# Expert v stage and FFN down projections with tokens stationary and 512 weight columns moving

## The chip, the cores and the metric

One core of one Trainium2 chip. The metric is the device time of one execution in microseconds (us), the median of several runs. A profile was taken of one further execution; in it all matrix work runs on PE (TensorE), elementwise work on DVE (VectorE), ACT (ScalarE) and POOL (GpSimd), and most transfers are issued by SP.

## What is computed

Two transformer blocks on 256 tokens of width 1024. The first has attention and then a PEER layer: for each token, 8 heads choose 16 of 16384 experts. The kernel computes it densely, as 128 groups of 128 experts:

```python
q = xc @ w_query; s = einsum(q, sub_keys); top-16 of each half, then top-16 of the sums
act = gelu(xc @ u_sel.T);   h = h + sum over chosen k of (g * act)[k] * v_sel[k]
```

The second block has a mixer (convolution, block attention, gated linear attention), a cross attention over 256 memory rows, and a gated FFN of width 2752 with a short convolution:

```python
x = x + hybrid_mixer(rmsnorm(x, norm_mix_g)); x = x + memory_cross_attention(rmsnorm(x), rmsnorm(mem))
x = x + conv_ffn(rmsnorm(x, norm_ffn_g))      # up, conv, silu(gate) * up, then @ w_down (2752 x 1024)
return rmsnorm(x, final_norm_g)               # x * rsqrt(mean(x * x) + eps) * gain
```

## The kernel before

**Units.** All weights come as units of 128 x 1024 fp32 numbers (512 KB). `unit()` loads one (`raw`), makes `wh`, its value rounded to fp32r (mostly on ACT), and `wl`, the rest (mostly on DVE; POOL in part of the u stage). Moving data is split in the same way (`ch`, `cl` or `ah`, `al`), and each product is three matmuls: high x high, high x low, low x high. There are 4 `raw` buffers and 3 each of `wh` and `wl`.

**Layout.** The residual `h1` lies by feature: 128 features on partitions, 8 feature blocks, 256 tokens along the free dimension. In most projections (`stat8`) a 128 x 128 weight block is stationary and 256 tokens move. A few (`by_token`: `mv`, `gv`, `go`) hold 128 tokens stationary and move the weight columns; for `mv` these are 512.

**Expert stages.** `u_unit(j)` computes one group's activations (24 matmuls). `v_unit(j)` multiplies them by the gates and adds their product with `v` to four PSUM banks, `acc`. A bank holds two feature blocks of 256 tokens; a v unit is 8 feature blocks of three matmuls, 24 in all. First 90 u units run, then pairs of v and u units for the other 38, then the last 90 v units. The gates of 8 groups are loaded at a time (`gate_load`, 1 MB).

**The joint.** After the last v unit four DVE instructions add `acc`, scaled by 1/2048, to `h1`; `gained` then makes `ah` and `al` from it (ACT and DVE, 8 each). In program order the memory's key and value projections (`xk`, `xv`) follow, then the norm's factor and the mixer's first projection, `glr`. `xk` and `xv` do not need `h1`.

**FFN.** 21 full steps `f` of two up units (`ua`, `ug`, 24 matmuls each) and, two steps later, the down unit `dn`, plus one half-filled step (`um`). `down_part` adds to four PSUM banks `facc` with the same form as `v_unit`. The last two down units run in parts, so that banks finish one after another.

**Tail.** Before: by feature, `facc` is added to `h1`, squared, summed over partitions by matmuls with a column of ones, turned into the root's inverse, spread over partitions by two transposes, multiplied with gain and factor, and stored in five pieces.

**Order.** Operations are recorded with priorities in program order (`fl.bias` shifts some), and `schedule()` places them by a greedy simulation with costs written in `_cost`; each engine then runs its own list in that order. All instructions are issued from one line (L681), so the profile is read by the names of tiles: `s` stands for every region of the areas s1, s2 and s3, `d`, `g`, `s`, `p` are also the names of the PSUM pairs, and `h` is `h1`.

Of the kernel before, what the change touches and what calls it, by code (L numbers as in the profile page):

```python
# [9 lines left out]
F32 = mybir.dt.float32  # L10
# [3 lines left out]
AF = mybir.ActivationFunctionType  # L14
OP = mybir.AluOpType
# [4 lines left out]
P = 128  # L20
NM = 16
T = 256
S = NM + T
D = 1024
KD = D // P
NEG = -1e30
FF = 2752
NF = 22
# [229 lines left out]
CST, EAR = {}, {}  # L258
# [4 lines left out]
        _o += _a.shape[1]  # L263


def _feat(x):

    return np.ascontiguousarray(x.T.reshape(KD, P, -1).transpose(1, 0, 2))


def pack(i):
    u = _units(i)
    st = np.empty((len(PLAN), P, 8, P), np.float32)
    for j, (name, m) in enumerate(PLAN):
        st[j] = u[name][m].reshape(P, 8, P)
    ks = i["peer_sub_keys"][0].reshape(16, P, P).transpose(2, 0, 1)
    c, e = _consts()
    return {
        "st": st,
        "xt": _feat(np.concatenate([i["meta_tokens"], i["x"][0]], 0)),  # L280
        "mt": _feat(i["mem_2"][0]),
        "sk": np.ascontiguousarray(ks),
        "vec": np.concatenate([a for _, a in _vec_list(i)], 1),
        "cst": np.concatenate(list(c.values()), 1),
        "ear": np.concatenate(list(e.values()), 1),
    }


# [403 lines left out]
def _build(tc, nc, ctx, A, O):  # L692
    fl = Flow(tc, nc)
    PE, V, SC, G, Q = fl.pe, fl.v, fl.s, fl.g, fl.q
# [18 lines left out]
    cst = one([P, A["cst"].shape[1]], F32, "cst")  # L713
    eps = one([P, 2], F32, "eps")
    h1 = one([P, KD, T], F32, "h1")
# [42 lines left out]
    def v_(name, j=0, n=1, rows=slice(None)):  # L758
        o = VEC[name][0] + j
        return vec[rows, o:o + n]  # L760

    def c_(name, rows=slice(None)):
        o, n = CST[name]
        return cst[rows, o:o + n]

    ident = c_("ident")

    def sm(n=8):
        return fl.tile([P, 32], F32, "sm")[:, :n]

    def bank(tag, name=None):
        return fl.tile([P, 512], F32, tag, name)
# [115 lines left out]
    r1, r2, r3 = area("s1"), area("s2"), area("s3", F32R)  # L888
# [9 lines left out]
    tmp = r2(4416)  # L898
    mask = r2(S)
    ear = tmp[:, 0:EAR["mask"][0]]  # L900
# [14 lines left out]
    mq = r1(8, T, back=0)  # L915
    old = r1.at[0]
    mk = r1(8, S)
# [14 lines left out]
    Q.dma_start(cst[:, :nc_], A["cst"][:, :nc_])  # L932
    pre.append(unit("kr"))
    Q.dma_start(ear, A["ear"][:, 0:EAR["mask"][0]])
    Q.dma_start(mask, A["ear"][:, EAR["mask"][0]:])
    oc = [bank("d")[:, :S] for j in range(2)]
    for j in range(2):
        stat8(oc[j], pre[j], nh, nl, ALL, True)
# [1 line left out]
    o = bank("g")  # L940
    total(o, squares(x, S, KD, 2), VC)
    r = sm(12)
# [22 lines left out]
    for half in range(2):  # L965
        a, b = slice(64 * half, 64 * half + 64), slice(64 - 64 * half, 128 - 64 * half)
# [511 lines left out]
    def v_unit(j, lo="v"):  # L1478
        if j == 0:
            acc.extend(bank(tag, "acc") for tag in "sspp")  # L1480
        if j % 8 == 0 and j < P - 16:
            gate_load(j // 8 + 2)
        if j % 2 == 0:
            g, e = divmod(j, 8)
            for i in range(2):
                a = slots(j + i).rearrange("p (b t) -> p b t", (P, NB16, 16), b=NB16)
                V.tensor_tensor(a, a, loaded[g][:, e + i], op=OP.mult)
        a = slots(j)
        ch, cl = fl.tile([P, T], F32R, "ch"), fl.tile([P, T], F32R, "cl")
        split(a, ch, cl)  # L1490
        wh, wl = unit("v", lo=lo)
        for d in range(8):
            o = acc[d // 2][:, (d % 2) * T:(d % 2 + 1) * T]
            PE.matmul(o, wh[:, d], ch, start=j == 0 and d % 2 == 0, stop=False, skip_group_check=True)
            PE.matmul(o, wh[:, d], cl, start=False, stop=False, skip_group_check=True)
            PE.matmul(o, wl[:, d], ch, start=False, stop=j == P - 1 and d % 2 == 1, skip_group_check=True)

    class Side:

# [58 lines left out]
    qz, at_ = r1(1024), r1(1024)  # L1558
    FULL = slice(0, T)

    for i in range(4):
        a = h1[:, 2 * i:2 * i + 2]
        V.scalar_tensor_tensor(a, acc[i].rearrange("p (a b) -> p a b", (P, 2, T), a=2), 1.0 / 2048, a, op0=OP.mult, op1=OP.add)
        for k in (2 * i, 2 * i + 1):
            gained(h1[:, k], v_("mix", k), ah[:, k], al[:, k])
    for j in range(2):
# [236 lines left out]
    SC.activation(rsb, rep, AF.Copy)  # L1803
    fl.bias -= BIAS[2]
    facc = [bank(tag, "facc") for tag in "sspp"]

    def up(name, dst, j, tag):

# [10 lines left out]

    held, down = {}, {}  # L1820

    def down_part(f, ds):
        ch, cl, n = held[f]
        wh, wl = down[f]
        for d in ds:
            o = facc[d // 2][:, (d % 2) * T:(d % 2 + 1) * T]
            for k, (a, b) in enumerate(((wh, ch), (wh, cl), (wl, ch))):
                PE.matmul(o, a[:n, d], b[:n], start=f == 0 and d % 2 == 0 and k == 0,
                          stop=f == NF - 2 and d % 2 == 1 and k == 2, skip_group_check=True)

    for name, f in FFN:
        w = tmp[:, 768 * (f % 4):768 * (f % 4) + 768]
        fa, fg, sg = w[:, :T], w[:, T:2 * T], w[:, 2 * T:3 * T]
        if name == "ua":
            up("ua", fa, f, "d")
        elif name == "ug":
            up("ug", fg, NF + f, "g")
            ch, cl = fl.tile([P, T], F32R, "ch"), fl.tile([P, T], F32R, "cl")
            held[f] = ch, cl, P
            last = gate(f, sg, fa, fg, slice(0, P), ch, cl)  # L1840
        elif name == "um":
            n = FF - WHOLE
            up("um", cu[:, 0], f, "d")
            Q.dma_start(cu[:n, 1], cu[n:2 * n, 0])
            held[f] = xh[:, 0], xl[:, 0], n
            gate(f, ca[:n, 0], cu[:n, 0], cu[:n, 1], slice(0, n), xh[:n, 0], xl[:n, 0])
        else:
            down[f] = unit("dn")
            if f < NF - 3 or f == NF - 1:
                down_part(f, range(8))  # L1850
    for ds in (range(4), range(4, 6), range(6, 8)):
        for f in (NF - 3, NF - 2):
            down_part(f, ds)

    r = sm(8)
    fl.hold = (last,)
    SC.activation(r[:, 2:3], c_("one"), AF.Sqrt)
    fl.hold = ()
    sq = [t.flat[:, 512 * j:512 * j + 512] for t in (mq, mk) for j in range(2)]
    o, order, sums = bank("g"), ((0, 2), (2, 2), (4, 2), (6, 1), (7, 1)), []  # L1860
    for k, n in order:
        a, b = h1[:, k:k + n], facc[k // 2][:, (k % 2) * T:(k % 2 + n) * T]
        added = V.tensor_tensor(a, b.rearrange("p (a b) -> p a b", (P, n, T), a=n), a, op=OP.add)
        q = sq[k // 2][:, (k % 2) * T:(k % 2 + n) * T]
        last = SC.activation(q.rearrange("p (a b) -> p a b", (P, n, T), a=n), a, AF.Square)
        if k == 2:
            V.tensor_add(sq[0], sq[0], q)
        elif k:
            sums += [q[:, j * T:j * T + T] for j in range(n)]
    fl.hold = (added,)  # L1870
    V.tensor_add(sq[0][:, :T], sq[0][:, :T], sq[0][:, T:])
    fl.hold = ()
    sums.append(sq[0][:, :T])
    for j, q in enumerate(sums):
        for c in range(2):
            PE.matmul(o[:, c:c + 1], q[:, TT[c]], c_("one"), start=j == 0 and c == 0, stop=j == len(sums) - 1 and c == 1,
                      skip_group_check=True)
    root = inv_sqrt(r[:, 0:2], o[:, 0:2], 1.0 / D, E1)
    rep = spread(r, 0, 1, QT)[:, :T]
    for k in range(KD):  # L1880
        fl.hold = (root if k > 2 else last,)
        SC.activation(h1[:, k], h1[:, k], AF.Copy, scale=v_("fin", k))
    fl.hold = ()
    for k, n in order:
        V.tensor_tensor(h1[:, k:k + n], h1[:, k:k + n],
                        rep.rearrange("p (o c) -> p o c", (P, 1, T), o=1).to_broadcast([P, n, T]), op=OP.mult)
        Q.dma_start(O["o"][:, k:k + n], h1[:, k:k + n])
    fl.emit()


_SHAPES = (("st", (len(PLAN), P, 8, P)), ("xt", (P, KD, S)), ("mt", (P, KD, T)), ("sk", (P, 16, P)), ("vec", (P, NVEC)),
           ("cst", (P, sum(n for _, n in CST.values()))), ("ear", (P, sum(n for _, n in EAR.values()))))


# [13 lines left out]
```

## Time and profile before

| | |
|---|---|
| Runs shown | 1358.08, 1359.37, 1361.27 us; median 1359.37 us |
| The profiled execution | 1356.64 us, of which the span from first to last instruction is 1354.6 us |
| Granted TensorE clock, mean over the span | 0.998 of 2.4 GHz |
| PE, DVE, ACT, POOL busy | 1333.6, 969.2, 722.3, 63.3 us |
| Matmuls | 11060 |
| HBM read | 236.33 MB |

The profile shows matmuls with their whole time in the pipeline, so neighbours overlap; the distance between starts has to be read from first and last start. Rows name the instruction as result<-operands with shapes; idle time before an instruction stands in brackets with what ended it.

### The profile page before, as it was taken

Reading aid. Unit: us, or ns where it says so; the run is one execution under the profiler, and the core shown is the slowest. Engines: PE = TensorE matmul, PEld = TensorE weight load, DVE = VectorE, ACT = ScalarE, POOL = GpSimd, SP = SyncE. Lnnn points to the kernel's source line nnn. Section 1 sums busy time; section 2 is a strip of 40 time slices with the busy share of each in tenths; the row PEclk is TensorE's granted clock in tenths of the full one; section 3 lists DMA queues with packets and bytes.
Section 4 is the critical chain, followed back from the end, with each engine's and each line's share of the span. In section 5 each row is a group of like instructions: output and inputs, shape, how many; then the busy total and the mean of one; then the engine's idle time right before and its main releaser. Section 6 shows DMA issues by size and latency. Waiting matters only on the chain.

```text
span 1354.6 us, 27185 instructions
## 1 busy us (share of the span) xinstructions
PE 1333.6 (98%) x11060; PEld 1292.8 (95%) x11060; DVE 969.2 (72%) x1832; ACT 722.3 (53%) x1219; POOL 63.3 (5%) x29
## 2 busy tenths in 40 slices
PE   9999999999999999999999999999999999999997
PEld 8898899999999999999999999999999797999997
DVE  7565889997598868975555555565576677878886
ACT  6445645445465665444444444455455646755555
POOL 0000001455100000000000000000000000000000
PEclk9999999999999999999999999999999999999999
DMA  6342344555587789996666565565555343466662
GB/s 237 120 138 79 116 150 143 166 189 187 161 290 265 257 274 351 358 342 193 186 186 184 184 184 185 186 202 187 178 181 172 93 142 123 127 202 186 183 186 85
DMA packets 101061, 255.99 MB, mean 189 GB/s; under 512 B 7940, under 2 KB 42952, under 8 KB 100808
## 3 DMA queue, kind: packets, MB, share of 16 engines
q1 hardware_dynamic: 95360, 236.36, 55.5%
q10 hardware_dynamic: 5576, 17.90, 3.3%
q8 instruction: 86, 1.41, 0.4%
q14 instruction: 39, 0.32, 0.1%
HBM read 236.33 MB, written 17.83 MB: 188 GB/s over the span
## 4 chain that ended last, share of the span: by engine, by line
PE 84%; DVE 8%; DMA 2%; ACT 1%; issue 1%; SPq 0%; DVEq 0%; ACTq 0%
PE d L681 29%; PE acc L681 25%; PE g L681 5%; PE facc L681 5%; PE ug L681 4%; PE ua L681 4%; DVE s L681 4%; PE s L681 3%; PE wq L681 3%; DVE wl L681 2%; DMA raw<-st 2%; PE p L681 2%; PE dq L681 1%; PE mq L681 1%; PE mk L681 1%
## 5 line engine op out<-in xcount | busy, mean ns | idle before, releaser
L681 ACT ACTIVATE wh<-raw 128x1024 fp32r<-128x1024 f32 x399 | 423.0, 1060 | 514.8 <-PE d L681 194.2
L681 DVE TENSOR_TENSOR wl<-raw,wh 128x1024 fp32r<-128x1024 f32 x385 | 474.6, 1234 | 268.3 <-ACT wh L681 266.2
L681 PE MATMUL d<-ah,wl 128*128 128x256 f32 x1088 | 308.4, 284 | 3.4 <-DVE wl L681 3.3
L681 PE MATMUL d<-ah,wh 128*128 128x256 f32 x1088 | 309.1, 284 | 0.4 <-DVE h L681 0.3
L681 PE MATMUL d<-al,wh 128*128 128x256 f32 x1088 | 307.7, 283 | 0.8 <-DVE al L681 0.8
L681 PE MATMUL acc<-cl,wh 128*128 128x256 f32 x1024 | 289.3, 283 | 0.0
L681 PE MATMUL acc<-ch,wh 128*128 128x256 f32 x1024 | 288.3, 282 | 0.0
L681 PE MATMUL acc<-ch,wl 128*128 128x256 f32 x1024 | 288.0, 281 | 0.0
L681 PEld LDWEIGHTS d<-ah,wl 128*128 128x128 f32 x1088 | 205.5, 189 | 5.9 <-DVE wl L681 4.8
L681 PEld LDWEIGHTS d<-ah,wh 128*128 128x128 f32 x1088 | 205.5, 189 | 1.7 <-DVE h L681 0.7
L681 PEld LDWEIGHTS d<-al,wh 128*128 128x128 f32 x1088 | 205.4, 189 | 1.6 <-DVE al L681 1.2
L681 PEld LDWEIGHTS acc<-cl,wh 128*128 128x128 f32 x1024 | 193.5, 189 | 0.0
L681 PEld LDWEIGHTS acc<-ch,wh 128*128 128x128 f32 x1024 | 193.1, 189 | 0.0
L681 PEld LDWEIGHTS acc<-ch,wl 128*128 128x128 f32 x1024 | 192.8, 188 | 0.0
L681 POOL TENSOR_TENSOR wl<-raw,wh 128x1024 fp32r<-128x1024 f32 x22 | 61.9, 2813 | 286.5 <-ACT wh L681 286.5
L681 DVE TENSOR_TENSOR cl<-s,ch 128x256 fp32r<-128x256 f32 x149 | 62.6, 420 | 11.6 <-ACT ch L681 11.6
L681 ACT ACTIVATE ch<-s 128x256 fp32r<-128x256 f32 x149 | 60.1, 404 | 12.4 <-PE acc L681 8.9
L681 DVE TENSOR_TENSOR s<-s,s 128x256 f32<-128x256 f32 (+5 forms) x142 | 55.3, 446 | 0.2
L681 DVE TENSOR_TENSOR s<-s 128x2048 f16<-128x2048 f16 (+4 forms) x48 | 53.8, 1122 | 0.8
L681 PE MATMUL d<-s,wh 128*128 128x256 f32 (+1 forms) x240 | 45.8, 292 | 3.3 <-ACT s L681 1.4
L681 PE MATMUL ua<-al,wh 128*128 128x256 f32 x168 | 47.7, 284 | 0.2 <-DVE al L681 0.2
L681 PE MATMUL ug<-ah,wl 128*128 128x256 f32 x168 | 47.6, 283 | 0.0
(301 smaller groups left out, 2406.9 us busy)
## 6 DMA issues: line engine op xcount, KB each, us to landing
raw<-st SPq DMA_DIRECT2D x407, 512.0 KB, 3.9
gd<-u ACTq DMA_DIRECT2D x32, 512.0 KB, 5.6
s<-gd SPq DMA_DIRECT2D x16, 1024.0 KB, 8.7
h<-xt SPq DMA_DIRECT2D x2, 512.0 KB, 7.9
s<-sk SPq DMA_DIRECT2D x1, 1024.0 KB, 5.2
u<-mt SPq DMA_DIRECT2D x4, 256.0 KB, 5.1
o<-h SPq DMA_DIRECT2D x3, 256.0 KB, 2.4
s<-ear SPq DMA_DIRECT2D x1, 664.0 KB, 6.0
```

Source lines behind the costliest of these rows:

```text
L681: f(*[real(a) for a in o.args], **{k: real(a) for k, a in o.kw.items()})
```

## The change

The v stage and the down projections swap roles: 128 tokens of `ch` or `cl` are stationary and 512 columns of `wh` or `wl` move. A unit becomes 12 matmuls instead of 24, and `acc` and `facc` hold tokens on partitions. At the joint `acc` is scaled into four regions `ys` (two on ACT, two on DVE), transposed back by 16 PE transposes into two `g` and two `s` banks, and added to `h1`. In the FFN, at f = 6, 8, 10 and 12, four transposes each bring `h1` to tokens (`hT`), with a copy by ACT. The final norm runs by token: an add, a square with a running sum on ACT, a root of one column, and multiplications by the gain (a new input region of 512 KB, `fin`, loaded at f = 4) and the factor. The output lies by token and is stored in four pieces of 256 KB, one of them on ACT's queue.

```diff
@@ v_unit
-        for d in range(8):
-            o = acc[d // 2][:, (d % 2) * T:(d % 2 + 1) * T]
-            PE.matmul(o, wh[:, d], ch, start=j == 0 and d % 2 == 0, stop=False, skip_group_check=True)
-            PE.matmul(o, wh[:, d], cl, start=False, stop=False, skip_group_check=True)
-            PE.matmul(o, wl[:, d], ch, start=False, stop=j == P - 1 and d % 2 == 1, skip_group_check=True)
+        for half in range(2):
+            rh, rl = (a[:, 4 * half:4 * half + 4].rearrange("p k c -> p (k c)", (P, 512)) for a in (wh, wl))
+            for c in range(2):
+                o = acc[2 * half + c]
+                PE.matmul(o, ch[:, TT[c]], rh, start=j == 0, stop=False)
+                PE.matmul(o, ch[:, TT[c]], rl, start=False, stop=False)
+                PE.matmul(o, cl[:, TT[c]], rh, start=False, stop=j == P - 1)
@@ the joint
+    ys = [tmp[:, 512 * i:512 * i + 512] for i in range(4)]
     for i in range(4):
+        if i % 2:
+            V.tensor_scalar(ys[i], acc[i], 1.0 / 2048, None, op0=OP.mult)
+        else:
+            SC.activation(ys[i], acc[i], AF.Copy, scale=1.0 / 2048)
+    for i in range(4):
+        o = bank("ggss"[i])
+        for k in range(2):
+            for c in range(2):
+                at = P * (2 * (i % 2) + k)
+                PE.transpose(o[:, T * k + P * c:T * k + P * c + P], ys[2 * (i // 2) + c][:, at:at + P], ident)
         a = h1[:, 2 * i:2 * i + 2]
-        V.scalar_tensor_tensor(a, acc[i].rearrange("p (a b) -> p a b", (P, 2, T), a=2), 1.0 / 2048, a, op0=OP.mult, op1=OP.add)
+        V.tensor_tensor(a, o.rearrange("p (a b) -> p a b", (P, 2, T), a=2), a, op=OP.add)
@@ down_part
-        for d in ds:
-            o = facc[d // 2][:, (d % 2) * T:(d % 2 + 1) * T]
-            for k, (a, b) in enumerate(((wh, ch), (wh, cl), (wl, ch))):
-                PE.matmul(o, a[:n, d], b[:n], start=f == 0 and d % 2 == 0 and k == 0,
-                          stop=f == NF - 2 and d % 2 == 1 and k == 2, skip_group_check=True)
+        for c, half in parts:
+            rh, rl = (a[:n, 4 * half:4 * half + 4].rearrange("p k c -> p (k c)", (n, 512)) for a in (wh, wl))
+            o = facc[2 * c + half]
+            for k, (a, b) in enumerate(((ch, rh), (ch, rl), (cl, rh))):
+                PE.matmul(o, a[:n, TT[c]], b, start=f == 0 and k == 0, stop=f == NF - 2 and k == 2)
@@ FFN loop, behind a down unit, and the last two down units
+            if f in (6, 8, 10, 12):
+                c, half = divmod(f // 2 - 3, 2)
+                o = bank("d")
+                for k in range(4):
+                    PE.transpose(o[:, P * k:P * k + P], h1[:, 4 * half + k, TT[c]], ident)
+                SC.activation(hT[2 * c + half], o, AF.Copy)
+            if f == 4:
+                Q.dma_start(fin, A["ear"][:, NEAR:])
-    for ds in (range(4), range(4, 6), range(6, 8)):
+    for part in FOUR:
         for f in (NF - 3, NF - 2):
-            down_part(f, ds)
+            down_part(f, (part,))
@@ the tail (all of the old one removed)
+    for c in range(2):
+        for i in (2 * c, 2 * c + 1):
+            V.tensor_tensor(hT[i], facc[i], hT[i], op=OP.add)
+            SC.activation(junk, hT[i], AF.Square, accum_out=r[:, i:i + 1])
+        for i in range(2 * c, 2 * c + 2 - c):
+            (V if c else G).tensor_mul(hT[i], hT[i], fin[:, 512 * (i % 2):512 * (i % 2) + 512])
+        V.tensor_add(r[:, 4 + c:5 + c], r[:, 2 * c:2 * c + 1], r[:, 2 * c + 1:2 * c + 2])
+        inv_sqrt(r[:, 6 + c:7 + c], r[:, 4 + c:5 + c], 1.0 / D, E1)
+    SC.activation(hT[2], hT[2], AF.Copy, scale=r[:, 7:8])
+    V.scalar_tensor_tensor(hT[3], hT[3], r[:, 7:8], fin[:, 512:], op0=OP.mult, op1=OP.mult)
+    for i in range(2):
+        V.tensor_scalar(hT[i], hT[i], r[:, 6:7], None, op0=OP.mult)
+    for i in range(4):
+        (SC if i == 2 else Q).dma_start(O["o"][:, i // 2, 512 * (i % 2):512 * (i % 2) + 512], hT[i])
```

## Rows read from the trace of the kernel before

**Rows 1.** Page: busy time of each engine, share of span, instructions.
```profile
span 1354.6 us, 27185 instructions
...
PE 1333.6 (98%) x11060; PEld 1292.8 (95%) x11060; DVE 969.2 (72%) x1832; ACT 722.3 (53%) x1219; POOL 63.3 (5%) x29
```

**Rows 2.** Busy time by stretch: engines, PEclk, DMA share, GB/s.
```profile
580.00:600.00 20.00, 19.97 (x168) 19.76 (x167) 16.29 (x28) 9.48 (x12) 0.00 (x0) 1.00 1.05 376
700.00:720.00 20.00, 20.00 (x171) 20.00 (x170) 10.93 (x15) 9.31 (x12) 0.00 (x0) 1.00 0.60 184
1100.00:1150.00 50.00, 46.82 (x343) 40.56 (x341) 39.45 (x89) 27.84 (x52) 0.00 (x0) 1.00 0.46 146
```

**Rows 3.** Tile view of `acc`, PE, 737 to 995 us: ns min/median/max, starts.
```profile
L681 PE MATMUL acc<-ch,wh x720: 278/282/363, 737.4 to 994.4; 128*128 128x256 f32 x180
...
L681 PE MATMUL acc<-ch,wl x720: 280/281/367, 737.6 to 994.6; 128*128 128x256 f32 x180
```

**Rows 4.** Timeline of PE, `mv` projection: start, duration, instruction.
```profile
1040.64 0.39 PE L681 MATMUL d<-wh,ah 128*128 128x512 f32 x1
...
1041.11 0.40 PE L681 MATMUL d<-wh,al 128*128 128x512 f32 x1
1041.35 0.40 PE L681 MATMUL d<-wh,ah 128*128 128x512 f32 x1
...
1051.57 0.40 PE L681 MATMUL d<-wh,al 128*128 128x512 f32 x1
```

**Rows 5.** Timeline of PE around six transposes in the u stage.
```profile
358.19 0.82 PE L681 MATMUL p<-cst,s 128*128 128x128 f32 x6
358.76 0.37 PE L681 MATMUL d<-ah,wh 128*128 128x256 f32 x1
```

**Rows 6.** Groups by shape from 990 us on: busy us, mean ns, idle before.
```profile
L681 DVE TENSOR_TENSOR wl<-raw,wh 128x1024 fp32r<-128x1024 f32 x106 | 129.4, 1222 | 30.3 <-ACT wh L681 29.7
...
L681 ACT ACTIVATION_READ_ACCUMULATOR s<-s,hs 128x1 f32 x16 | 3.0, 189 | 0.0
...
L681 DVE SCALAR_TENSOR_TENSOR h<-acc,h 128x512 f32<-128x512 f32 x4 | 2.6, 686 | 1.4 <-PE acc L681 1.4
...
L681 ACT ACTIVATE s<-p 128x512 f32<-128x512 f32 x4 | 2.4, 598 | 1.8 <-PE p L681 1.8
...
L681 ACT ACTIVATE s<-h 128x512 f32<-128x512 f32 x3 | 1.9, 632 | 1.2 <-DVE h L681 1.2
```

**Rows 7.** Chain that ended last, 990 to 1016 us: start, us, what.
```profile
995.39 1.80 DVE h L681 x3
997.19 2.37 DVE al L681 x6
...
999.90 1.14 DVE wl L681
...
1007.05 3.09 PE glr L681 x24
```

**Rows 8.** Timeline of PE at the first `xv` unit.
```profile
1001.08 0.39 PE L681 MATMUL d<-wl,s 128*128 128x256 f32 x1 [0.33 <-DVE wl L681]
```

**Rows 9.** Timeline of all engines, the tail.
```profile
1344.66 0.28 PE L681 MATMUL facc<-ch,wl 128*128 128x256 f32 x1
...
1347.44 0.26 ACT L681 ACTIVATE sm<-g,eps 128x2 f32<-128x2 f32 x1
...
1347.74 0.17 DVE L681 RECIPROCAL sm<-sm 128x2 f32<-128x2 f32 x1 [1.67 <-ACT sm L681]
...
1348.42 2.55 DVE L681 TENSOR_TENSOR h<-h,g 128x512 f32<-128x512 f32 x5 [0.52 <-PE g L681]
1349.19 2.48 SPq L681 DMA_DIRECT2D o<-h  x5
```

**Rows 10.** Timeline of POOL and DVE, 272 us.
```profile
272.22 2.38 POOL L681 TENSOR_TENSOR wl<-raw,wh 128x1024 fp32r<-128x1024 f32 x1 [5.07 <-ACT wh L681]
...
272.67 3.00 DVE L681 TENSOR_TENSOR wl<-raw,wh 128x1024 fp32r<-128x1024 f32 x1
```

More of the change, by code (lines that the diff above doesn't have):

```diff
@@ L263 @@
         _o += _a.shape[1]
+NEAR = sum(n for _, n in EAR.values())
 def _feat(x):
@@ L284, in pack @@
         "cst": np.concatenate(list(c.values()), 1),
-        "ear": np.concatenate(list(e.values()), 1),
+        "ear": np.concatenate(list(e.values()) + [np.tile(np.reshape(i["final_norm_g_2"], (1, D)), (P, 1))], 1),
     }
@@ L934, in _build @@
     Q.dma_start(ear, A["ear"][:, 0:EAR["mask"][0]])
-    Q.dma_start(mask, A["ear"][:, EAR["mask"][0]:])
+    Q.dma_start(mask, A["ear"][:, EAR["mask"][0]:NEAR])
     oc = [bank("d")[:, :S] for j in range(2)]
@@ L1805, in _build @@
     facc = [bank(tag, "facc") for tag in "sspp"]
+    FOUR = [(c, half) for c in range(2) for half in range(2)]
+    r2 = area("s2")
+    hT, fin, junk = [r2(512) for _ in range(4)], r2(D), r2(512)
     def up(name, dst, j, tag):
@@ L1820, in _build, with down_part @@
     held, down = {}, {}
-    def down_part(f, ds):
+    def down_part(f, parts):
         ch, cl, n = held[f]
         wh, wl = down[f]
-        for d in ds:
-            o = facc[d // 2][:, (d % 2) * T:(d % 2 + 1) * T]
-            for k, (a, b) in enumerate(((wh, ch), (wh, cl), (wl, ch))):
-                PE.matmul(o, a[:n, d], b[:n], start=f == 0 and d % 2 == 0 and k == 0,
-                          stop=f == NF - 2 and d % 2 == 1 and k == 2, skip_group_check=True)
+        for c, half in parts:
[3 more added lines that the diff above has]
+                PE.matmul(o, a[:n, TT[c]], b, start=f == 0 and k == 0, stop=f == NF - 2 and k == 2)
     for name, f in FFN:
@@ L1849, in _build @@
             if f < NF - 3 or f == NF - 1:
-                down_part(f, range(8))
-    for ds in (range(4), range(4, 6), range(6, 8)):
+                down_part(f, FOUR)
+            if f in (6, 8, 10, 12):
[6 more added lines that the diff above has]
+                Q.dma_start(fin, A["ear"][:, NEAR:])
@@ L1852, in _build @@
+    for part in FOUR:
         for f in (NF - 3, NF - 2):
-            down_part(f, ds)
-    r = sm(8)
+            down_part(f, (part,))
+    r = sm(16)
     fl.hold = (last,)
-    SC.activation(r[:, 2:3], c_("one"), AF.Sqrt)
+    SC.activation(r[:, 12:13], c_("one"), AF.Sqrt)
     fl.hold = ()
[L1859 to L1887, printed above, removed]
+    for c in range(2):
[6 more added lines that the diff above has]
+        inv_sqrt(r[:, 6 + c:7 + c], r[:, 4 + c:5 + c], 1.0 / D, E1)
@@ L1888, in _build @@
+    SC.activation(hT[2], hT[2], AF.Copy, scale=r[:, 7:8])
[4 more added lines that the diff above has]
+        (SC if i == 2 else Q).dma_start(O["o"][:, i // 2, 512 * (i % 2):512 * (i % 2) + 512], hT[i])
     fl.emit()
 _SHAPES = (("st", (len(PLAN), P, 8, P)), ("xt", (P, KD, S)), ("mt", (P, KD, T)), ("sk", (P, 16, P)), ("vec", (P, NVEC)),
-           ("cst", (P, sum(n for _, n in CST.values()))), ("ear", (P, sum(n for _, n in EAR.values()))))
+           ("cst", (P, sum(n for _, n in CST.values()))), ("ear", (P, NEAR + D)))
@@ L1901 @@
     ins = {n: nc.dram_tensor(n, s, F32, kind="ExternalInput").ap() for n, s in _SHAPES}
-    outs = {"o": nc.dram_tensor("o", (P, KD, T), F32, kind="ExternalOutput").ap()}
+    outs = {"o": nc.dram_tensor("o", (P, 2, D), F32, kind="ExternalOutput").ap()}
     with tile.TileContext(nc) as tc:
@@ L1906 @@
     o = r.results[0]["o"]
-    return np.ascontiguousarray(o.transpose(2, 1, 0).reshape(1, T, D))
+    return np.ascontiguousarray(o.transpose(1, 0, 2).reshape(1, T, D))
```

## The prediction

> **What bounds the kernel now.** I read the page first. Its first part shows PE busy for 98% of the span [rows 1]. Matmuls are pipelined, so that figure alone does not say that PE is the limit. The next view was the busy time by stretches. In 700 to 720 us (expert v stage) PE is busy all 20 us at granted clock 1.00, which is the 2.4 GHz level, while DVE and ACT are busy about half of the time and the DMA engines 60% [rows 2]. Nothing but PE can set the pace there. In 580 to 600 us the DMA engines are at 1.05 and DVE at 16.3 of 20 us, and PE still loses only 0.03 us [rows 2]. So the question for this stage is how far apart matmuls start, not how long each is shown.
>
> The tile view of `acc` gives that distance. Between 737.4 and 994.6 us there are 3 x 720 matmuls of 256 columns, nothing else of size on PE [rows 3]: 257.2 us over 2159 steps is 119.1 ns. A few small matmuls for the memory's norm lie in between; I take 118.9 ns. Each is shown with 282 ns, so more than two are in flight.
>
> The trace of before already holds the new form. The second block's `mv` projection has token columns stationary and 512 weight columns moving, the same fp32r tiles, the same order of operands. Its 48 matmuls start from 1040.64 to 1051.57 us [rows 4]: 10.93 us over 47 steps is 232.6 ns. Two narrow ones cost 237.8 ns, so one wide one in place of a pair saves **5.2 ns**, about 2%. That is the whole gain of the matmul part.
>
> **The change part by part.**
>
> *Expert v stage.* 128 units of 24 matmuls become 128 of 12: 1536 pairs x 5.2 ns = **-8.0 us**. The split work per unit on ACT and DVE, and the 512 KB load, stay as they are, and a unit only shrinks from 2.85 to 2.79 us, so their cover stays.
>
> *In the stretch with full DMA engines* (520 to 600 us, four windows like the one shown [rows 2], where the 1 MB gate loads share the queue with the weight loads) a faster PE may just wait for weights. Of its units, 5.7 us for a u and a v, some 14 are v units, worth 14 x 62 ns = 0.9 us. I give back **+0.4** (0 to 0.9).
>
> *Down projections.* 22 units of 24 matmuls become 12 each: 264 pairs x 5.2 ns = **-1.4 us**. It is the same form with another output bank.
>
> *Transposes.* New are 16 after the v stage (scaled sums back to features) and 16 inside the FFN (h1 to tokens). In the trace six transposes between two weight matmuls take from 358.19 to 358.76 us, 0.095 us each [rows 5]. 32 x 0.095 = **+3.0 us**, all on PE. The bounds are 1.5, if those after the v stage fill time in which PE would wait (next part), and 3.8, if each costs a quarter more.
>
> *The four FFN transposes' banks* come from the two that `ua` uses, and ACT empties each in 0.6 us [rows 6]. With two banks an up projection can start late: **+0.2** (0 to 0.8). The 512 KB load of the final gain goes on SP among weight loads at f = 4, with DMA engines about 60% busy in the comparable stretch; I cost it at nothing (a queue that runs dry would cost up to its own 1.4 us, 512 KB at the 376 GB/s of rows 2).
>
> *The joint between the blocks.* Here the chain runs through DVE, not PE: adds of `h`, then `al`, then `wl` of the `xv` unit at 999.90 us, which PE awaits [rows 7]. PE's `d` matmul starts at 1001.08 after a wait [rows 8]. Before, one of the four adds ran ahead of the last v matmul. Now nothing can be added before the transposes, so four adds of 0.69 us [rows 6] stand behind the end of the v stage, and two scaled copies of acc (one 0.6 to 0.7 us on DVE behind the end) stand ahead of them. That is 1.4 us more on DVE, and up to 2.5 with the round through PE. The 16 transposes fill 1.5 us of PE in the same place. Behind the wait are `xv` and `glr`; `glr` starts at 1007.05 [rows 7] and has its inputs seven us early, so it hides the rest. I take **+0.8** (-0.6, when transposes fill the wait, to +2.5).
>
> *The tail.* Before, the last down matmul starts at 1344.66 and ends near 1344.94; the span ends at 1354.6, so the tail is 9.7 us [rows 9, 1]: 20 sum matmuls, root, spread, five multiplies, five stores. Now the last part needs one add 0.69, one square 0.63 with an accumulator read 0.19, a small add 0.1 (an estimate, under the reciprocal's 0.17), root 0.26, reciprocal 0.17, last multiply 0.69 [rows 6, 9], that is 2.73, plus six hand-offs of 0.05 us: 3.0. From the last multiply (1350.97) to the end it was 3.6 us, with a 128 KB store last [rows 9]. Two 256 KB stores side by side land a little later, so I take 3.9. New tail 6.9, a gain of 2.7. Against it stands the first token half. Its two gain multiplies go to POOL, and the second half's one on DVE also reads two SBUF tensors. The trace shows what that does: a DVE subtraction of this kind, 1.22 us on the mean [rows 6], took 3.00 us when POOL was inside a 2.38 us one [rows 10]. Half-sized ones on POOL are 1.2 us each. If DVE is caught, the small add queued behind it, and then root and stores, come up to 1.2 us late. I take 0.5 of it: **-2.2 us** (-3.2 to -1.0).
>
> On this the Trainium skill, page "SBUF — State Buffer", section "Who interferes with whom", says that a DVE instruction with two SBUF inputs and a GpSimd instruction that reads SBUF exclude each other, the later one blocking fully; the trace agrees with 3.00 us. By that rule alone the tail would gain 1.5 instead of 2.2.
>
> Sum: -8.0 + 0.4 - 1.4 + 3.0 + 0.2 + 0.8 - 2.2 = **-7.2 us**. The profiled execution took 1356.64 us (span 1354.6 and 2.0 around it), so it would take 1349.4. The three runs have a median of 1359.37, 2.7 us above it; -7.2 from there is **1352.2 us**, 0.53% faster. About 0.2% (2.7 us) is what a measurement of this kernel can tell from no change.
>
> **Rivals.**
>
> *A smaller fixed share per matmul.* If the 118.9 ns are nearly all per column and the `mv` rows flatter the wide form (48 only, with lighter work beside them), a pair saves about half, 2.5 ns: 1800 x 2.5 = 4.5 instead of 9.4 us, sum -2.3, 1357.1 us: no change. Against it: 47 steps are steady. The Trainium skill, page "TensorE: Matmul & The Clock Gate", section "Back-to-back issue gap", gives N/2.4 + 2.5 ns for a warm matmul, so 109.2 and 215.8 ns here; the trace has 118.9 and 232.6 and so differs in both. Its rule puts the saving at this rival's 2.5 ns per pair. Chance 0.07.
>
> *The wide matmul is slower than two narrow ones.* Every eighth or so of the `mv` steps takes 0.24 us (1041.11 to 1041.35 [rows 4]). If busier DVE, ACT and DMA in the v stage made that the rule, 1800 x (241 - 237.8) = +5.8 in place of -9.4: sum +8.0, 1367 us: slower. It decides from 236.6 ns per wide matmul on, where all is even. Against it: the mean there is 232.6 with weight loads running. Chance 0.05.
>
> *Order behind the joint.* All engine orders come from one list schedule over the whole program. A different joint can reorder the second block's dependent stretch, where PE already stands idle 3.2 of 50 us (1100 to 1150 us [rows 2]). Doubling that costs 3 us, and with a joint at its upper bound (+1.7) the sum is -2.5; a worse order, 5 to 8 us, would give 1357 to 1361. Chance 0.16, about half still faster.
>
> *More than forecast.* The transposes fit into the joint's wait and the tail gains its 3.2 us: sum near -10.5, 1349 us. Chance 0.10.
>
> **How the numbers follow.** Forecast 0.62, its own range 1349.5 to 1355; rivals 0.07, 0.05, 0.16, 0.10. Faster by over 0.2% (below 1356.6): 0.62 + 0.10 + half of 0.16 = 0.80. Within: 0.07 + 0.05 of the order case = 0.12. Slower: 0.05 + 0.03 = 0.08. The range is 1347.5 to 1357: its low end takes nearly every lower bound, its high end the first rival and the milder order case; what is left out on both sides is under 0.2.
>
> **What would show it.** In the `acc` rows: 512 columns, 1536 matmuls, starts 232 to 233 ns apart and the v stage about 8 us shorter (236.6 or more would make the first step wrong). At the joint: 16 transposes in about 1.5 us and a PE wait before `xv` under 1.5 us. In the FFN: groups of four transposes costing about 0.4 us. In the tail: 7 to 8 us from the last `facc` matmul to the end, and a look at whether DVE's multiply stretches beside POOL. The prediction is wrong if the step is near 238, or if PE's idle time between 1000 and 1160 us grows by more than 4 us.

## The result, and the profile after

Before: 1359.3 us, median of 4 runs (1358.08 to 1361.27). After: 1350.87 us, median of 4 (1350.25 to 1353.38). The ratio is 0.994 with a 95% interval of 0.9923 to 0.9957, so 0.6% faster, inside the predicted range and 1.3 us below the predicted time. The profiled execution of after took 1350.25 us, 6.4 less than that of before; the medians lie 8.4 apart, because before's profiled execution was 2.7 us quicker than its median and after's only 0.6.

The page of after, where [rows 1] are the same lines of before:

```profile
span 1348.3 us, 23744 instructions
...
PE 1325.5 (98%) x9270; PEld 1203.2 (89%) x9270; DVE 979.5 (73%) x1833; ACT 722.3 (54%) x1222; POOL 66.1 (5%) x31
```

PE is still busy for 98%. PEld fell from 95 to 89%, since in the v stage and the down projections half as many weight loads serve the same columns.

For the rest I cut the span at the first and last starts of matmuls on named tiles: the v stage from the first to the last `acc` matmul, the joint from there to the first `glr`, the FFN from the first `ua` to the last `facc`, the tail from there to the end. These lengths (us) come from the traces' own starts, and the step is the mean distance between neighbouring `acc` starts in the last 90 v units, without the three distances in which six small matmuls of the memory's norm lie.

| | before | after | difference | forecast |
|---|---|---|---|---|
| up to the v stage | 518.69 | 518.51 | -0.18 | 0 |
| v stage | 475.90 | 469.84 | **-6.06** | -7.6 |
| joint | 12.45 | 13.96 | +1.51 | +2.3 |
| first `glr` to first `ua` | 148.87 | 148.88 | +0.01 | 0 |
| FFN | 188.74 | 188.93 | +0.19 | +0.3 |
| tail | 9.96 | 8.17 | -1.79 | -2.2 |
| span | 1354.62 | 1348.30 | -6.32 | -7.2 |
| step per 512 columns, ns | 237.7 | 233.8 | -3.9 | -5.2 |

(The forecast column groups the terms of the prediction: v stage -8.0 + 0.4; joint 1.5 of transposes + 0.8; FFN -1.4 + 1.5 + 0.2.)

The tile view of `acc` in the last 90 v units, columns as in [rows 3]:

```profile
L684 PE MATMUL acc<-wh,ch x360: 388/397/482, 735.6 to 987.9; 128*128 128x512 f32 x180
L684 PE MATMUL acc<-wl,ch x360: 389/400/400, 735.8 to 988.1; 128*128 128x512 f32 x180
L684 PE MATMUL acc<-wh,cl x360: 387/396/475, 736.1 to 988.4; 128*128 128x512 f32 x180
```

1080 matmuls, from 735.6 to 988.4 us: 252.8 us over 1079 steps is 234.3 ns, and 233.8 without the three steps with small matmuls inside. The forecast was 232 to 233.

The same three stretches as in [rows 2], with the DMA-full one taken whole:

```profile
520.00:600.00 80.00, 78.86 (x499) 70.63 (x498) 71.52 (x140) 39.65 (x52) 0.00 (x0) 1.00 1.05 357
700.00:720.00 20.00, 20.00 (x124) 17.82 (x124) 11.63 (x16) 9.62 (x13) 0.00 (x0) 1.00 0.57 188
1100.00:1150.00 50.00, 46.68 (x336) 40.25 (x337) 38.04 (x89) 29.91 (x58) 0.00 (x0) 1.00 0.37 127
```

At granted clock 1.00 PE fills 700 to 720 us, so nothing but PE sets that pace. In 1100 to 1150 us it is busy for 46.68 us (46.82 before): the order behind the joint did not get worse. From 520 to 600 us it is busy for 78.86 of 80 us; the same window of before gave 79.56 us.

The chain that ended last, at the joint (start, us, what), beside [rows 7]:

```profile
984.83 3.93 PE acc L684 x17
988.76 0.22 PE g L684 x2
988.98 0.02 issue
988.99 0.87 PE g L684 x6
989.87 0.87 PE s L684 x8
990.74 5.75 PE xk L684 x48
996.49 5.76 PE d L684 x48
...
1002.32 0.71 PE glr L684 x4
```

Before, this chain ran through DVE (`h`, `al`, `wl`) and PE waited at `xv` [rows 8]. Now it is PE from end to end: 16 transposes in 2.0 us, then `xk` and `xv` back to back. The wait is gone, and the transposes stand where it was.

The tail on all engines, beside [rows 9]:

```profile
1338.84 2.53 POOL L684 TENSOR_TENSOR s<-s 128x512 f32<-128x512 f32 x2 [988.60 <-ACT s L684]
...
1339.77 0.38 DVE L684 TENSOR_TENSOR sm<-sm 128x1 f32<-128x1 f32 x1
...
1340.13 0.39 PE L684 MATMUL facc<-wh,cl 128*128 128x512 f32 x1
...
1340.56 0.69 DVE L684 TENSOR_TENSOR s<-facc,s 128x512 f32<-128x512 f32 x1 [0.41 <-PE facc L684]
...
1341.34 0.63 ACT L684 ACTIVATE s<-s 128x512 f32<-128x512 f32 x1 [0.49 <-DVE sm L684]
...
1341.88 0.19 ACT L684 ACTIVATION_READ_ACCUMULATOR s<-s 128x1 f32 x1
1342.23 0.15 DVE L684 TENSOR_TENSOR sm<-sm 128x1 f32<-128x1 f32 x1
...
1342.41 0.29 ACT L684 ACTIVATE sm<-sm,eps 128x1 f32<-128x1 f32 x1 [0.35 <-DVE sm L684]
1342.74 0.17 DVE L684 RECIPROCAL sm<-sm 128x1 f32<-128x1 f32 x1
...
1342.94 0.75 DVE L684 SCALAR_TENSOR_TENSOR s<-s,sm 128x512 f32<-128x512 f32 x1
1343.69 0.37 ACTq L684 DMA_DIRECT2D o<-s  x1
```

From the last add's start (1340.56) to the last multiply's end (1343.69) it takes 3.13 us, against 3.0 forecast. From there to the end of the span it takes 4.61, against 3.9. The DMA view of the last nine us (issues, size, median us to landing) shows why:

```profile
o<-s SPq DMA_DIRECT2D x3, 256.0 KB, 2.9
o<-s ACTq DMA_DIRECT2D x1, 256.0 KB, 3.3
```

256 KB takes about 3 us to land with the other queue moving at the same time: the last landing comes 3.29 us after the last multiply (2.71 before). The span ends 1.32 us later still (0.94 before; 0.8 to 1.3 in the runs here).

### The profile page after: what moved, and what is told of

It reads as the page before. It is cut to its first block, busy times and chain, and to the rows that moved or that the text cites. A ratio compares the mean times of both kernels' runs of the same rounds, so it can differ in the third digit from the quotient of the medians.

```text
span 1348.3 us, 23744 instructions
## 1 busy us (share of the span) xinstructions
PE 1325.5 (98%) x9270; PEld 1203.2 (89%) x9270; DVE 979.5 (73%) x1833; ACT 722.3 (54%) x1222; POOL 66.1 (5%) x31
## 4 chain that ended last, share of the span: by engine, by line
PE 83%; DVE 8%; DMA 2%; ACT 2%; issue 1%; SPq 0%; ACTq 0%; DVEq 0%
PE d L684 28%; PE acc L684 25%; PE g L684 5%; DVE s L684 5%; PE ua L684 4%; PE ug L684 4%; PE facc L684 4%; PE s L684 3%; PE wq L684 3%; DVE wl L684 3%; DMA raw<-st 2%; PE p L684 2%; PE dq L684 1%; PE mk L684 1%; PE mq L684 1%
## 5 line engine op out<-in xcount | busy, mean ns | idle before, releaser
L684 PE MATMUL acc<-wh,ch 128*128 128x512 f32 x512 | 203.4, 397 | 0.0
L684 PE MATMUL acc<-wl,ch 128*128 128x512 f32 x512 | 203.0, 397 | 0.0
L684 PE MATMUL acc<-wh,cl 128*128 128x512 f32 x512 | 202.3, 395 | 0.0
L684 PEld LDWEIGHTS acc<-wh,cl 128*128 128x128 f32 x512 | 96.5, 188 | 23.4
L684 PEld LDWEIGHTS acc<-wh,ch 128*128 128x128 f32 x512 | 96.5, 188 | 22.6
L684 PEld LDWEIGHTS acc<-wl,ch 128*128 128x128 f32 x512 | 96.4, 188 | 21.5
L684 ACT ACTIVATE s<-d 128x512 f32<-128x512 f32 (+1 forms) x71 | 41.4, 583 | 14.9 <-PE d L684 14.9
```

The costliest lines, as they stand in the source:

```text
L684: f(*[real(a) for a in o.args], **{k: real(a) for k, a in o.kw.items()})
```

## The experiments

Edits are given in short form, not line by line.

**The two halves apart.** `v_only` has the change in the v stage and the joint, `down_only` the rest (down projections, their transposes, the tail).

```diff
v_only: v_unit and the joint of after, everything from `facc` on as before
down_only: v_unit and the joint of before, everything from `facc` on as after
```

> The expert v stage and the joint as in the changed kernel, the down projections and the tail as before. Width theory (a wide matmul replaces two narrow ones and saves about 4.5 ns): the v stage, first to last acc start, takes 470 us as in the changed kernel (before 475.9), the joint to the first glr matmul 14.0 (before 12.5), the rest is unchanged; 4 to 5 us faster than before. Rival (the gain of the change is mostly its shorter tail and the v stage gives nothing): no faster than 1 us.

> The down projections, the transposes in the FFN and the tail as changed, the v stage and the joint as before. Width theory: the FFN from its first up matmul to the last facc start stays within 0.5 us of before (264 pairs save 1.2, 16 transposes cost 1.5 to 1.6, a wait before the last down unit 0.6), and the tail gives 1.8; 1.5 to 2 us faster than before. Rival (the tail carries the whole change): 5 us or more faster.

Measured, beside 1359.46 us for before in the same runs: `v_only` 1353.22 us, ratio 0.9956 (0.9945 to 0.9967); v stage 470.07, step 233.79, joint 13.96, tail 9.87. `down_only` 1357.55 us, ratio 0.9985 (0.9975 to 0.9995); v stage 476.68, joint 12.46, FFN 189.09, tail 7.65. The parts add up (6.2 + 1.9 = 8.1 us of medians, 8.4 for the whole): the v stage brings 5.8 and its joint takes 1.5; the down projections give nothing once their transposes are paid (+0.35), and their gain is the tail's 2.3.

**Is it the width?** `v_256` keeps the new roles, the tiles and their buffers, and cuts each 512-column matmul in two. `v_order` keeps the width and changes only the order.

```diff
v_256
+            for c in range(2):
+                for q in range(2):
+                    rh, rl = 256 columns of wh, wl from block 4 * half + 2 * q
+                    o = acc[2 * half + c][:, 256 * q:256 * q + 256]
+                    PE.matmul(o, ch, rh); PE.matmul(o, ch, rl); PE.matmul(o, cl, rh)
v_order, for each c
+            for half in range(2):
+                PE.matmul(acc[2 * half + c], ch, rh[half]); PE.matmul(acc[2 * half + c], ch, rl[half])
+            for half in range(2):
+                PE.matmul(acc[2 * half + c], cl, rh[half])
```

> The changed kernel with tokens stationary in the v stage but only 256 weight columns moving in one matmul, 24 per unit; nothing is left out. Width theory: steps of 118.9 ns return, the v stage takes 476 us, 6 us more than the changed kernel, which leaves it 2 to 3 us faster than before. Orientation rival (what helps is that tokens are stationary): the v stage stays at 470 us and the total within 1 us of the changed kernel.

> The changed kernel with another order in a v unit: four matmuls in a row on the same stationary ch, then two on cl, with the bank changing between them. Width theory: only the columns count, steps stay at 233.5 to 234.5 ns and the v stage at 470 us. Rival (a repeated stationary operand or a steady bank matters): steps change by 1 ns or more, the v stage by 1.5 us or more.

Tile view of `acc` in `v_256`, whole v stage:

```profile
L684 PE MATMUL acc<-wh,ch x1024: 279/279/364, 519.7 to 985.6; 128*128 128x256 f32 x171
...
L684 PE MATMUL acc<-wh,cl x1024: 274/276/366, 519.9 to 985.9; 128*128 128x256 f32 x171
```

and in `v_order`:

```profile
L684 PE MATMUL acc<-wh,ch x512: 388/392/481, 519.9 to 985.0; 128*128 128x512 f32 x171
...
L684 PE MATMUL acc<-wh,cl x512: 387/394/481, 520.8 to 985.7; 128*128 128x512 f32 x171
```

`v_256` issues twice the matmuls and needs less time for them: v stage 466.20 us, step 115.67 ns, that is 231.3 per 512 columns, 2.5 below the wide form. Its median is 1348.28 us (1346.58 to 1354.42), ratio 0.9935 (0.9914 to 0.9957); that overlaps with after's 0.9923 to 0.9957, so it is the steps that tell the two apart and not the totals. `v_order` has 231.28 per wide matmul and a v stage of 465.78 (one run, 1347.34 us). My theory, that a wide matmul saves a fixed share of a narrow one, falls: the same columns at half the width are no slower.

Nor does the order settle it, for after reaches the same step with its own order. Its tile view of `acc`, first and last rows of 900 to 949.5 us and of 955 to 990 us:

```profile
L684 PE MATMUL acc<-wh,cl x71: 387/396/402, 899.7 to 948.9; 128*128 128x512 f32 x71
L684 PE MATMUL acc<-wl,ch x71: 392/400/400, 900.2 to 949.3; 128*128 128x512 f32 x71
...
L684 PE MATMUL acc<-wh,ch x49: 388/388/397, 954.6 to 987.9; 128*128 128x512 f32 x49
L684 PE MATMUL acc<-wh,cl x49: 394/397/401, 955.1 to 988.4; 128*128 128x512 f32 x49
```

Up to 950 us the wide matmuls start 234.1 ns apart, from 955 us on 231.1 (from the traces' own starts; the rows are rounded). Instructions, order and tiles are the same; between the two lie the norm's six small matmuls, from 950 to 953 us. All six executions with this form of the v stage that were profiled (after, `v_only`, `no_joint`, `no_ffn_t`, `tail_order`, `tail_dve`) have 234.07 before these and 231.09 behind them. So one stream of instructions has more than one pace, and an interruption can move it from one to the other; `v_order` has 231.1 on both sides.

**Is it how often the stationary operand repeats?** In `v_256` two neighbouring groups of three matmuls hold the same tokens. In `v_alt` no two neighbouring groups do; `v_max` lets `ch` stand for eight matmuls and `cl` for four. `v_alt` also changes the order of operands in `stat8`.

```diff
v_alt, 256 columns
+        for c, half, q in ((0,0,0), (1,0,1), (0,1,0), (1,1,1), (0,0,1), (1,0,0), (0,1,1), (1,1,0)):
+            (ch, rh), (ch, rl), (cl, rh)
in stat8: (wh, xh), (wh, xl), (wl, xh)  becomes  (wh, xh), (wl, xh), (wh, xl)
v_max, 256 columns, for each c
+            for q in range(4): (ch, rh[q]), (ch, rl[q])
+            for q in range(4): (cl, rh[q])
```

> Two edits whose places do not meet. (1) The v stage with tokens stationary and 256 columns moving, but the token halves alternate from triple to triple, so that no stationary operand comes back in the next triple and no moving operand is repeated back to back. If what made the 256-column form fast is that a stationary operand comes back in the next triple: steps return to 118.5 to 119 ns from 115.7, and the v stage to about 475 us. If what slows the other forms is a moving operand repeated back to back, or if it is only the place of the operands: steps stay at 115.5 to 116 ns, 466 us. (2) In the projections with weights stationary (u stage, ups) the order is high x high, low x high, high x low, so that the moving operand stays for two matmuls and the stationary one changes each time. If a repeated stationary operand saves time: the u steps rise from 119.1 to 121 ns or more. If the order does not matter there: 118.8 to 119.4 ns.

> The v stage with 256 columns moving and the stationary operand kept as long as it goes: eight matmuls on one ch, then four on its cl. If a stationary operand that comes back saves time: steps of 115 ns or less (from 115.7), v stage 464 us or less. If the order within the triple makes the difference: steps between 115.7 and 119 ns, 466 to 476 us.

`v_alt` keeps 115.66 ns without reuse between groups, `v_max` has 117.86 with the most. So reuse is not what pays (the two `ch` matmuls within a group stand together in all forms; that was not varied). In the u stage the other order gained nothing: 400 to 500 us has 120.0 ns per step in `v_alt` as in after. From 230 to 340 us after has 118.7 and `v_alt` 119.5; but `v_order`, in which nothing of the u stage was changed, has 120.0 there, so that too is a matter of pace. (The totals of these single runs are 1355.92 and 1353.74 us: `v_max`'s is that of its step, with a v stage of 472.84 us; `v_alt`'s also carries waits, see below.)

**Is it where the operands lie?** `v_place` is `v_256` with the `ch` and `cl` tiles 64 bytes longer, so these and the tiles placed behind them move, by how much was not recorded; every instruction is the same.

```diff
-        ch, cl = fl.tile([P, T], F32R, "ch"), fl.tile([P, T], F32R, "cl")
+        ch, cl = (fl.tile([P, T + 16], F32R, n)[:, :T] for n in ("ch", "cl"))
```

> The kernel with 256 moving columns by token (steps of 115.67 ns in its last 90 v units), instruction for instruction, with the buffers of ch and cl 64 bytes longer, so that all of them and of wh and wl lie at other addresses, each of the three ch buffers at another offset. If the addresses of the operands decide (a conflict of reads): the step moves by 1 ns or more, or the units differ by buffer by 10 ns or more. If they do not: 115.5 to 115.9 ns, v stage 466 us, equal for the three buffers.

PE's timeline at 800 us in `v_256`, the first and the thirteenth of a row (start, duration):

```profile
799.95 0.28 PE L684 MATMUL acc<-wh,ch 128*128 128x256 f32 x1
...
801.33 0.28 PE L684 MATMUL acc<-wh,ch 128*128 128x256 f32 x1
```

and in `v_place`:

```profile
799.73 0.28 PE L684 MATMUL acc<-wh,ch 128*128 128x256 f32 x1
...
801.15 0.28 PE L684 MATMUL acc<-wh,ch 128*128 128x256 f32 x1
```

Twelve steps take 1.38 us in the one and 1.42 in the other. Over the 90 units the step is 118.13 ns instead of 115.67, the v stage 477.69 us instead of 466.20. In both traces the steps repeat with the position in the unit and with the buffers that it got, in turns of three: `v_256` has 118, 116 and 112 to 113 ns everywhere, `v_place` mostly 119, 121, 113 in one set of buffers and 117 to 119 in another. The two differ by 4.9 ns per 512 columns, more than the 3.9 of the whole change. `v_place` is one execution, and one stream can have two paces. For the placement speaks that the norm's small matmuls and the u units in between leave both as they are: 115.5 to 116.1 ns on all sides in `v_256` and `both_256`, 117.9 to 118.1 in `v_place`. And in the down projections, where `v_place` has after's instructions, its median unit has 231.6 ns per matmul, against 234.8 or 234.9 in all ten other runs with that form: there the moved tiles are the quicker ones. The Trainium skill, page "SBUF — State Buffer", section "Who interferes with whom", knows only the port that DVE and GpSimd share as a place of contention, and says that PE waits for no other engine. No run here shows what it is in the addresses that PE's step depends on, so none speaks for or against that.

The longer v stage of `v_place` has a second part, in the DMA-full stretch. Windows of `v_256` and `v_place`, and two of `v_alt`:

```profile
520.00:600.00 80.00, 78.83 (x668) 78.21 (x667) 72.90 (x144) 39.63 (x53) 0.00 (x0) 1.00 1.08 369
```

```profile
520.00:600.00 80.00, 75.88 (x628) 74.47 (x626) 68.85 (x141) 36.75 (x51) 0.00 (x0) 1.00 1.11 343
```

```profile
520.00:600.00 80.00, 73.91 (x598) 72.17 (x597) 68.54 (x140) 37.13 (x51) 0.00 (x0) 0.98 1.05 346
532.70:536.10 3.40, 3.40 (x19) 3.40 (x18) 2.46 (x6) 2.52 (x4) 0.00 (x0) 0.50 1.10 371
```

PE stands idle for 4.1 us in `v_place` instead of 1.2 while the queue brings 343 GB/s instead of 369. `v_alt`, with `v_256`'s step, loses 6.1 us there (73.91 busy). It waits for weights in both. In `v_alt` one wait is 2.99 us long, for a weight load that landed late (ACT awaited it for 5.96 us), and 1.9 us after it the granted clock fell to 0.50 for 3.4 us, in which matmuls started 214 ns apart instead of 119.

**The joint.** `no_joint` leaves out the conversion of layout behind the v stage.

```diff
-    (ys, 16 transposes, add of the transposed bank)
+        V.scalar_tensor_tensor(a, acc[i].rearrange(...), 1.0 / 2048, a, op0=OP.mult, op1=OP.add)
```

> The changed kernel without the scaled copies and the 16 transposes behind the v stage: acc is added to h1 by the four instructions of before, so that the conversion of layout is left out. If the joint costs what the traces show (16 transposes 1.7 us, less a wait before the memory's value projection that they fill): from the last acc start to the first glr start 12.4 us instead of 14.0, and 1.4 to 1.7 us off the span. Rival (the transposes are hidden and the joint's price is DVE's longer chain): the wait for wl of that projection is gone too and it saves under 0.7 us, or over 2.5 us if both add up.

Tile view of `acc` in `no_joint`, and then PE's timeline at its `xv` unit:

```profile
L684 PE MATMUL acc<-wh,cl x512: 387/396/475, 521.5 to 992.0; 128*128 128x512 f32 x171
```

```profile
998.66 0.39 PE L684 MATMUL d<-wl,s 128*128 128x256 f32 x1 [0.41 <-DVE wl L684]
```

From the last `acc` start, 992.0, to the first `glr`, 1004.6, it is 12.63 us instead of 13.96. The conversion costs 1.33 us, less than the 2.0 that its transposes take on PE, because without them a wait before `xv` is back (0.41 us, the rest of the difference was not traced). What DVE and ACT do for it does not show on after's chain.

**The FFN's transposes.** `no_ffn_t` copies `h1` without transposing it, so leaves out that change of layout.

```diff
-                (bank, four transposes, copy from it)
+                SC.activation(hT[2 * c + half].rearrange("p (k c) -> p k c", (P, 4, P), k=4), h1[:, 4 * half:4 * half + 4, TT[c]], AF.Copy)
```

> The changed kernel with the 16 transposes in the FFN left out: ACT copies the untransposed values of h1 to the same places, so that only the change of layout is missing. If PE sets the pace of the FFN: from the first up matmul to the last facc start 1.4 to 1.9 us less than the changed kernel (16 x 0.09 to 0.12). Rival (the d bank that they take delays up projections as well): 2.2 us or more less.

The FFN takes 186.79 us, 2.14 less. Of that 1.42 are the transposes (four groups of three steps at 109 ns and one at 28), 0.49 lie in the up units (`ua` 0.39, `ug` 0.10), 0.25 in the last wait, next. PE's timeline of after at the first group shows what most of the 0.39 is:

```profile
1230.29 0.60 PE L684 MATMUL d<-cst,h 128*128 128x128 f32 x4
1230.65 0.36 PE L684 MATMUL ua<-ah,wh 128*128 128x256 f32 x1
1230.85 0.28 PE L684 MATMUL ua<-al,wh 128*128 128x256 f32 x1
```

The first `ua` matmul behind the transposes holds the next one off for 200 to 203 ns, where it has 112 to 119 without them: 0.35 us in the four groups. So a transpose costs about 0.11 us in all, and 16 some 1.8. That the total lies between the two expectations is no sign of a price for the banks: at most 0.15 us is left for it.

**The end of the FFN.** PE's timeline of after, before the last down unit:

```profile
1335.23 0.40 PE L684 MATMUL facc<-wh,cl 128*128 128x512 f32 x1
1336.07 0.50 PE L684 MATMUL facc<-wh,ch 128*128 128x512 f32 x1 [0.44 <-ACT ch L684]
```

A step of 0.84 us where 0.23 is normal: PE has done the first quarter of the last but one down unit and awaits the last one's gate (`ch`, from ACT). Before, the same place took 0.29 us. `tail_order` gives PE three quarters of the earlier unit first, `tail_dve` moves the first half's two gain multiplies from POOL to DVE.

```diff
tail_order: parts as (step f, part)
-    (19,0) (20,0) (19,1) (20,1) (19,2) (20,2) (19,3) (20,3)
+    (19,0) (19,1) (19,2) (20,0) (20,1) (19,3) (20,2) (20,3)
tail_dve
-            (V if c else G).tensor_mul(hT[i], hT[i], fin[...])
+            V.tensor_mul(hT[i], hT[i], fin[...])
```

> The changed kernel with a third part of the second last down unit put ahead of the last unit's first part. Theory: the 0.84 us between two facc starts at 1335.2 us is a wait for the last gate's ch; another 0.7 us of work ahead of it closes it to 0.3 us or less, and as the first token half still ends two parts before the end, the tail stays 8.1 to 8.4 us: 0.4 to 0.6 us faster than the changed kernel. Rival (the first token half's norm then runs into the second's on ACT): the tail grows by as much, no change.

> The changed kernel with the two gain multiplies of the first token half on DVE instead of POOL. POOL theory (POOL's 1.26 us multiplies hold DVE up in the tail, as the first token half's small add of 0.38 us shows): that add takes 0.15 us, and the tail gets 0.2 to 0.5 us shorter. Rival (only instructions off the path that sets the end are held up, and DVE's two multiplies of 0.69 us now stand in front of its adds): the tail stays within 0.2 us or grows by up to 0.7.

`tail_order`: ratio 0.9945 (0.9927 to 0.9962), 1351.88 us. FFN -0.69, tail +0.52: the wait closes, but the two token halves now finish so close together that their norms queue on DVE: its reciprocal for the second half stands behind two scalings of the first. That is the rival's course; nothing is gained. `tail_dve`: ratio 0.9948 (0.9933 to 0.9964), 1351.79 us. The small add that stood 0.38 us beside POOL now takes 0.15:

```profile
1342.83 0.15 DVE L684 TENSOR_TENSOR sm<-sm 128x1 f32<-128x1 f32 x1
```

Yet the chain from the last `facc` matmul to the last multiply is 3.67 us, not shorter than 3.56. The tail's -0.38 lies behind the last landing (1.32 to 0.84 us). So POOL does hold DVE, off the path; that it costs time here is not shown, since the edit also puts DVE's multiplies ahead of the last add, which now starts 0.55 us after the last `facc` start instead of 0.43.

**Together.** `both_256` takes the narrow form of `v_256` in the down projections too, and `tail_dve`'s edit.

```diff
+            for q in range(2):
+                rh, rl = 256 columns of wh, wl;  o = facc[2 * c + half][:, 256 * q:256 * q + 256]
+            V.tensor_mul(hT[i], hT[i], fin[...])
```

> The 256-column form by token in the down projections as well, and the two gain multiplies of the first token half on DVE: the version that the runs point to. If the gain of that form carries over (231.3 instead of 233.7 ns for 512 columns): the FFN's down part gives 0.6 us, the tail 0.2 to 0.4, so 4 to 5 us faster than the changed kernel in the profile's span, 1346 to 1348 us, 0.8 to 0.95% faster than before. If it does not carry over: the FFN stays at 188.6 to 189.0 us and the total within 0.5 us of the kernel with 256 columns in the v stage alone.

```profile
L684 PE MATMUL acc<-wh,ch x1024: 278/279/364, 519.7 to 984.9; 128*128 128x256 f32 x171
```

1345.35 us (1344.37 to 1346.42), ratio 0.99 (0.9878 to 0.9921) against before, so below after's interval too. v stage 465.49, step 115.66, FFN 188.63, tail 7.17. In the down projections its median unit has 116.3 ns per step (232.6 per 512 columns; 234.8 in after). Over after the v stage gives 4.4 us, the tail 1.0 and the FFN 0.3; 1.2 are lost in the stretch ahead, where nothing was edited.

## Why the prediction was right, and what in it was not

The time and the sign hold, and the stages change in the directions forecast. That the size came out so near (-6.3 us between the profiles, -8.4 between the medians, for -7.2) is in part luck: the step was read from a place that happened to have a pace near that of the v stage, and the misses in the v stage (1.5 us too much gained) and at the joint (0.8 too much lost) have opposite signs. By its own steps:

*Expert v stage, -8.0.* The mechanism's place is right, the size is not: "one wide one in place of a pair saves 5.2 ns" measured 3.9 (237.7 to 233.8), and 1536 x 3.9 = 6.0 is what the stage gave. The step that failed is the one behind it, "That is the whole gain of the matmul part": I read the `mv` rows as a property of 512 columns. `v_256` and `v_order` show that half the width, or another order, gives 231.3, `v_place` that the same instructions as `v_256`'s cost 236.3 with tiles moved, and after itself that its own stream goes from 234.1 to 231.1. The `mv` rows were the price of one place and pace, not of a width. On the mean of the v stage or of `mv` wide matmuls took 231.3 to 233.8 ns here and pairs of narrow ones 231.3 to 240.0 (the u stage, 400 to 500 us), and single down units with wide ones 231.0 to 240.7; so the ranges overlap, and that the width as such gains anything is not shown.

*Rivals for the matmul.* "Smaller fixed share" (2.5 ns per pair) and the forecast (5.2) stand about equally far from 3.9; neither mechanism is borne out. That rival's rule from the Trainium skill, page "TensorE: Matmul & The Clock Gate", section "Back-to-back issue gap", gives 109.2 and 215.8 ns, and the section says that it holds for a single matmul by itself, which I left out. No stage of any run here came near, the lowest mean of one kind of step being 112.7 (`v_256`). "Wide is slower than two narrow" is out against before; `v_256` is quicker than after's mean, but no quicker than after's last 35 us of the stage.

*DMA-full stretch, +0.4.* The 38 mixed pairs gained 1.59 us where 456 pairs x 3.9 = 1.8 were on offer, so 0.2 was given back. PE waits there for weights, as said.

*Down projections -1.4, transposes and banks +1.7.* Sum +0.19 instead of +0.3, by errors that cancel: the stretches of `facc` became 0.81 us shorter, since a wait of 0.84 us before the last unit that I had not foreseen took half a us; the transposes took 1.42; the up units, which I had 0.2 longer, came out 0.41 shorter, though the first matmuls behind the transposes add 0.35 to them. Why they are shorter was not looked into. The price of a transpose, 0.095 us, was too low by that same piece: behind the six of [rows 5], too, the next matmul has a step of 201 ns instead of 119, which makes it 0.109 each.

*Joint, +2.3.* It was 1.5. The bound that I named and did not take, that transposes fill PE's wait, is what happened: the chain holds no DVE piece, and `no_joint` saves 1.33. By that bound the joint would have been +0.9 (1.5 - 0.6); the transposes took 2.0 us where I had 1.5.

*Tail, -2.2.* It was -1.8. The compute part was right (3.13 for 3.0). The stores were the miss: 4.61 us from the last multiply for 3.9, of which 3.29 to the last landing and 1.32 behind it. DVE was caught by POOL (0.38 us), without a cost that a run shows.

*Order behind the joint.* 148.88 us from `glr` to `ua` against 148.87: unchanged in after and within 0.2 us of that in all experiments but `no_joint`, where it is 1.2 longer. There 0.3 is a longer wait at 1102.91 us; the rest falls between 1135 and 1149 us, where the granted clock was at half for 3.5 us:

```profile
1143.70:1147.20 3.50, 3.42 (x14) 2.19 (x15) 1.13 (x6) 1.88 (x5) 0.00 (x0) 0.51 0.00 0
```

**What stays open.** What sets PE's step was not found. It differs with the order of the operands and with their placement, each seen in single runs, and within one execution with nothing changed but an interruption; so the cause of the v stage's gain, 3.9 ns per pair, is open, and only its place is shown. Why a weight load comes late in the DMA-full stretch, so that one run loses 1 us there and another 6, is not settled either. `v_256`'s own five runs spread from 1346.58 to 1354.42 us, so single runs were read by their steps and stages, not by their totals. Part of such spread goes with the clock: the stretch ahead of the v stage took 518.5 us in after, where the granted clock stayed at 1.00, 519.7 in `v_256` and 521.0 in `tail_dve`, whose profiles have one and two pieces of 3.4 us at 0.50 there.

## What to carry to other kernels

A step between matmuls that another place of the same kernel shows is the price of that place's tiles, buffers, order and pace too; before it is put down to a shape, run the shape at half the size with all else kept, and see whether the step changes within one execution. Where PE is the bound and units repeat over rotating buffers, the runs here have steps 2% apart (231.3 to 236.3 ns per 512 columns) for the same work in another order or placement; both are cheap to try. New PE work is cheapest where PE waits anyway: 16 transposes at the joint hold PE for 2.0 us and cost 1.3.

## What was not expected of the hardware

- The same instructions at two paces in one execution: 234.1 ns per wide matmul up to six small matmuls in between, 231.1 behind them.
- The same instructions on moved tiles: 118.13 ns per 256-column matmul instead of 115.67, locked to the position in the unit and the buffer (one run).
- With another order: 233.79 to 231.28 ns per 512 columns, 115.67 to 117.86 per 256 (one run each).
- Of four fp32 transposes in a row among weight matmuls, three take 109 ns each and the step behind the fourth is 28; but the matmul behind them has a step of 200 to 203 ns instead of 112 to 119.
- A 128 x 1 add took 0.38 us on DVE beside a POOL multiply, 0.15 without.
